# Neighbourhood attention in a two-layer encoder: both heads of a pair go through each query block together, and the keys wrap around

## The chip, the cores and the metric

The kernel runs on one core of one Trainium2 chip. The metric is the device time of one execution in microseconds (us). Three runs of the kernel before took 1664.18 to 1666.24 us, with a median of 1666.17 us. A profile of one execution goes with them, and its times are counted from the start of its span. Engines are named as in the profile: PE is TensorE's matrix multiplication and PEld its loading of weights (the stationary operand), DVE is VectorE, ACT ScalarE, POOL GpSimd, and SP the queue that issues most DMAs.

## The reference, cut to what matters

The model is an encoder of two layers over 512 tokens on a grid of 8 rows and 64 columns, with 1024 features in fp32. Layer 0 is neighbourhood attention and a dense SwiGLU, layer 1 latent attention (MLA) and a mixture of experts; each part is preceded by a modulated norm. The part at issue is the neighbourhood attention, with 16 heads of 64 features:

```python
q, k, v = split(h @ w_qkv); q = q * 64 ** -0.5
# every token sees 8 rows x 16 columns around its own, clamped at the border
s = q . k(window) + rpb[head, row offset, column offset]
p = softmax(s)            # over the 128 keys of the window
o = (p . v(window)) @ w_o
```

The modulation vectors of all parts come from `silu(c) @ w_ada + b_ada`, and a part of this product runs beside the attention.

## The kernel before, in words

Every fp32 matrix product with weights is made of three passes over a high and a low part of each operand ("hi" and "lo", lines 295 to 297, tiles `mm`, one accumulation of 24 matmuls of 512 columns for a projection). Weights arrive by DMA as `raw` tiles; ACT casts the high part (L195) and DVE subtracts for the low part (L198). DVE also sums the background product with `w_ada` (L225, `ada_acc`).

The tokens are ordered so that a window of 16 columns lies within 256 consecutive positions. So a query block of 128 positions needs 256 keys, and there are four query blocks (b = 0 to 3). The last block's keys wrap from position 511 to 0. Before the change a key tile `kT` has 640 columns, and POOL copies its first 128 columns behind the 512 (L749). Keys hold the high parts in partitions 0 to 63 and the low parts in 64 to 127. Queries `qH` hold the high part twice, the copy made by POOL (L741), and `qL` the low part over zeros, so two matmuls make a score.

Two heads form a pair, and there are eight pairs in four groups. The generator `attend(pair)` does, for head h and block b:

- PE: two matmuls of 256 columns into the score tile `s` (L682);
- DVE: adds bias and mask `mb` and takes the minimum along the row into `nm` (L685; scores carry a minus sign);
- ACT: exponential with the row sum `den` (L688); DVE: reciprocal (L689) and product (L690);
- PE: two transposes into `pt` (L693); ACT: a copy to `pT` (L695);
- PE: two matmuls `po` of a 128 x 64 block of V with `pT` (L697). Each stands in the trace as two records of 128 columns, so one head's block has four. Head 0 writes partitions 0 to 63 of `po`, head 1 partitions 64 to 127, so the two heads use different halves of PE's columns (form 128*64; all else in this stage has form 128*128).

All eight (head, block) steps of a pair come one after another in the code, head 0 first. POOL makes three `mb` tiles for each head (first, inner and last block, L674) from masks and the bias table `rb`, which SP loads (L628). Tiles live in pools with a fixed number of buffers: `s`, `pt`, `pT` and `mb` have two, `e`, `nm` and `den` three. The projections of the next group are issued between the pairs. Outside the start of this stage and the expert stage a scheduler sets the order of the instructions on each engine when the program is built: it sorts ready work by its own estimates, so attention steps and projection matmuls alternate on PE. On the chip each engine then works through its list in that order. After the last pair the output projection `na_o` (reading `oH` and `oL`) follows, then the dense SwiGLU. The latent attention of layer 1 has a product of the same form, `po` in L956, with 512 columns.

Of the kernel before, what the change touches and what calls it, by code (L numbers as in the profile page):

```python
# [13 lines left out]
OP = mybir.AluOpType  # L14
# [44 lines left out]
class Kernel:  # L59
# [20 lines left out]
    def add_slots(self, pool, n, big, raw_pool, n_raw):  # L80
        """slots besides the standing ones: for split weights n of pool and some of the big tiles, for loads n_raw and
        the halves of a big tile"""
        self.extra = pool
        self.slots = ["split"] * N_SPLIT + ["extra"] * n + ["big"] * big
        self.raw_slots = [raw_pool] * n_raw + [0, 1] + [self.rawp] * N_RAW
        self.turn_no, self.raw_no = N_FIRST - 1, -1
# [4 lines left out]
    # ---------------------------------------------------------------- weights  # L91
    def add_split(self, key, srcs, nk, cols, perm=None):
        """srcs: list of (dst column, DRAM AP [nk*128 rows, cols])."""
        self.jobs.append(("split", key, srcs, nk, cols, perm))
# [5 lines left out]
    def need(self, key, ahead=1):  # L100
        """Emit loads and splits up to `ahead` split jobs past `key`."""
# [25 lines left out]
    def preload(self, n, limit=None):  # L127
        """loads of the next n jobs"""
# [55 lines left out]
    def pieces(self, hi, lo, raw, early=0):  # L184
        """high and low parts, 1024 columns at a time; early: all high parts first, with a pause after them"""
# [25 lines left out]
    # -------------------------------------------------------------------- ada  # L211
# [20 lines left out]
    def ada_finish(self, acc, layer, which, m0, n):  # L232
        """sums over the partitions of acc [128, n * 128] -> columns m0 .. m0 + n of one modulation vector"""
# [16 lines left out]
    def emit_ada_cols(self, layer, which, b, raw=None):  # L250
        """256 columns of one modulation vector at a time"""
# [29 lines left out]
    # -------------------------------------------------------------- utilities  # L281
    def proj(self, hi, lo, m, act_hi, act_lo, nk, cols=P, tok=ALL):
        """psum[cols features, tokens] = W^T act, three exact passes."""
# [24 lines left out]
    def rstd_steps(self, accs, tok=ALL, eng=None):  # L308
        """pairs of [128, tokens], n -> self.rstd: PSUM [128, tokens] of each, 1/sqrt(sum over the partitions / n + eps)
        on every partition; pauses where TensorE would wait"""  # L310
# [42 lines left out]
    def norm_steps(self, xT, layer, which, hi, lo, tok):  # L353
        """hi + lo = modulated norm of the finished x"""
# [23 lines left out]
    def finish(self, xT, key, act_hi, act_lo, nk, layer, which, norm, ahead=None):  # L378
        """x += g * W^T act. The last outputs come in two halves of the tokens: the norm of one half runs under the
        products of the other."""  # L380
# [33 lines left out]
    # ------------------------------------------------------------------ setup  # L414
# [20 lines left out]
    def plan(self):  # L435
        """The order in which weights stream through the core."""
# [53 lines left out]
    def split_swapped(self, hi, lo, src):  # L490
        """last axis: exchange the members of each pair"""
# [29 lines left out]
    # ------------------------------------------------ neighbourhood attention  # L521
    def na_phase(self):
        nc, tc, d = self.nc, self.tc, self.d
        with ExitStack() as es:
# [15 lines left out]
            def gate():  # L540
                """sums for half the modulation of 256 features; loads run a fixed number of jobs ahead"""
                self.emit()
                self.preload(N_LOADS, N_GATES)
# [15 lines left out]
            def weights():  # L559
                """high parts now, the rest later"""  # L560
# [50 lines left out]
            vp = pool("na_v", 3)  # L611
            w2 = pool("na_w2", 2)
# [48 lines left out]

            def attend(pair):
# [3 lines left out]
                po = ps_o.tile([P, S], F32, name="po")  # L666
                for h in range(2):
                    rb = RB[pair][:, h, 248:249]
                    MB = []
                    for v in range(3):  # L670
                        mb = w2.tile([P, 256], F32, name=f"mb{v}")
# [6 lines left out]
                    for b in range(4):  # L678
                        z = qz[pair % NQ][h]
                        s = ps_s.tile([P, 256], F32, name="s")  # L680
                        for i in range(2):
                            nc.tensor.matmul(s, z[i][:, b * P:(b + 1) * P], kT[h][:, b * P:b * P + 256], start=i == 0, stop=i == 1)  # L682
                        e = w3.tile([P, 256], F32, name="e")
                        nm = w3.tile([P, 1], F32, name="nm")
                        nc.vector.tensor_tensor_reduce(e, s, MB[0 if b == 0 else (2 if b == 3 else 1)],  # L685
                                                       op0=OP.add, op1=OP.min, scale=1.0, scalar=3e38, accum_out=nm)
                        den = w3.tile([P, 1], F32, name="den")
                        nc.scalar.activation(e, e, AF.Exp, bias=nm, scale=-1.0, accum_out=den)  # L688
                        nc.vector.reciprocal(den, den)  # L689
                        nc.vector.tensor_scalar_mul(e, e, den)  # L690
                        pt = ps_t.tile([P, 2, P], F32, name="pt")
                        for t in range(2):
                            nc.tensor.transpose(pt[:, t], e[:, t * P:(t + 1) * P], self.ident)  # L693
                        pT = w2.tile([P, 2, P], F32, name="pT")
                        nc.scalar.copy(pT, pt)  # L695
                        for t in range(2):
                            nc.tensor.matmul(po[h * 64:h * 64 + 64, b * P:(b + 1) * P],  # L697
                                             V[:, (b + t) % 4, h * 64:h * 64 + 64], pT[:, t],
                                             start=t == 0, stop=t == 1)
                        yield  # L700
# [31 lines left out]
    def na_query(self, ps, z):  # L732
        """scaled queries of two heads, 64 positions on: the high parts twice, the low parts over zeros"""
# [9 lines left out]
    def na_key(self, ps, kp):  # L743
        """keys of two heads, high parts over low parts"""
        nc = self.nc
        kT = [kp.tile([P, 640], F32R, name=f"kT{h}") for h in range(2)]
        for h, k in enumerate(kT):
            self.split_piece(k[0:64, 0:512], k[64:128, 0:512], ps[h * 64:h * 64 + 64])
            nc.gpsimd.tensor_copy(k[:, 512:640], k[:, 0:128].bitcast(F32))  # L749
# [7 lines left out]
    # ------------------------------------------------------------- dense ffn  # L757
# [58 lines left out]
    # ------------------------------------------------ latent attention  # L816
    def mla_phase(self, xT, hH, hL, norm):
        nc, tc, d = self.nc, self.tc, self.d
        scale = 96.0 ** -0.5
        with ExitStack() as es:  # L820
# [20 lines left out]
            def latent(psums, tok):  # L841
                """norms of the compressed queries and keys"""
# [123 lines left out]
    # ------------------------------------------------ mixture of experts  # L966
# [13 lines left out]
    def router(self, small, hp, ps_a, ps_b, ps_c, cst):  # L980
        """generators that make the choice of experts from the halves of hT"""
# [41 lines left out]
        def first_rows(onehot, idx0, cnt):  # L1023
            """counts, places of the tokens among their experts' rows, and the rows of the first expert's first block"""
# [20 lines left out]
        def rest(R, C, T, idx0, ps_y):  # L1045
            """the rows of the first expert's second block, weights, every expert's rows, and the rows that each token
            reads back"""
# [72 lines left out]
    def moe_phase(self, xT, oH, oL):  # L1120
        nc, tc, d = self.nc, self.tc, self.d
        with ExitStack() as es:
# [84 lines left out]
            def part(x, ks, b, z, n=P):  # L1207
                """columns of block b: P high parts and P low parts, of few rows FEW and FEW"""
# [61 lines left out]
            def few_rows(ps, x, w, k0, k1, nk):  # L1270
                """high and low parts of at most FEW rows side by side: two passes, the sums of the low parts in partitions FEW on"""
# [27 lines left out]
            def overflow():  # L1299
                """slots past the first CAP of every expert, added to x_tok"""  # L1300
# [71 lines left out]
            def second_block(n, many, few):  # L1372
                """one of two ways for the rows past the first P"""
# [23 lines left out]
            def emit_to(n):  # L1397
                """splits of the first n jobs"""
# [28 lines left out]
            def flush():  # L1427
                """what ScalarE and VectorE still owe the second block"""
# [292 lines left out]
```

## Time and profile before

| | |
|---|---|
| median of three runs | 1666.17 us |
| profiled execution, span | 1664.0 us |
| granted TensorE clock, mean | 0.989 of full speed |
| PE busy | 1591.8 us (96%) |
| DVE busy | 1110.5 us (67%) |
| ACT busy | 825.3 us (50%) |
| POOL busy | 311.5 us (19%) |
| attention of layer 0 in the span | first score 77.2 us, last `po` 262.8 us |

The span runs from the first to the last instruction of the program; the median of the runs is 2.2 us above it. Matmuls are pipelined: a matmul of 512 columns lasts 0.39 us in the records while the next one starts 0.23 us after it. So the cost of PE work is read from start to start, not from durations, and a PE shown as busy can still lose time between two starts.

### The profile page before, as it was taken

The numbers are of one execution on the slowest core, as the hardware profiler recorded it, in microseconds if no ns is written. First come the engines' busy times: TensorE is split into PE (matmuls) and PEld (weight loads), VectorE is DVE, ScalarE is ACT, GpSimd is POOL, SyncE is SP. The second block draws the span as 40 slices with busy tenths as digits, with TensorE's granted clock in tenths as the row PEclk, the third lists the DMA queues.
The fourth block names the chain that finished last, engine by engine and source line by source line (L and its number), as shares of the span: only waits on it lengthen the run. The fifth ranks groups of instructions, "written<-read, shape, count | busy, mean of one in ns | idle before, by whom it ended". The sixth has DMA issues, their size and how long they took to land. (4 is left out here: it accounts for less than half of the span.)

```text
span 1664.0 us, 23262 instructions
## 1 busy us (share of the span) xinstructions
PE 1591.8 (96%) x7909; PEld 1258.5 (76%) x7909; DVE 1110.5 (67%) x1720; ACT 825.3 (50%) x1416; POOL 311.5 (19%) x275
## 2 busy tenths in 40 slices
PE   6899999999999999989999989999999999999996
PEld 4777778988888888966568677778887777777885
DVE  5777855755554624788874768755546888887765
ACT  3455543522122123477673657545446767766442
POOL 0342210001000000012100353212112333333310
PEclk9999999999999999999999989999999999999998
DMA  9635431357655523312213399858558999997851
GB/s 354 195 114 173 161 127 52 130 199 247 224 176 178 177 72 112 102 59 69 67 35 107 140 346 355 271 189 271 169 183 297 333 354 355 339 371 264 261 190 52
DMA packets 241210, 327.39 MB, mean 197 GB/s; under 512 B 9586, under 2 KB 191570, under 8 KB 240404
## 3 DMA queue, kind: packets, MB, share of 16 engines
q1 hardware_dynamic: 231072, 296.19, 53.5%
q0 software_dynamic: 5232, 18.09, 3.1%
q10 hardware_dynamic: 4740, 11.02, 1.8%
q8 instruction: 89, 1.46, 0.4%
q14 instruction: 77, 0.63, 0.1%
HBM read 308.75 MB, written 16.52 MB: 195 GB/s over the span
## 5 line engine op out<-in xcount | busy, mean ns | idle before, releaser
L198 DVE TENSOR_TENSOR lo<-raw,hi 128x1024 fp32r<-128x1024 f32 (+1 forms) x284 | 375.2, 1350 | 96.5 <-ACT hi L195 88.1
L195 ACT CAST hi<-raw 128x1024 fp32r<-128x1024 f32 (+1 forms) x319 | 318.5, 1045 | 220.7 <-PE mm L296 142.0
L296 PE MATMUL mm<-hL,hi 128*128 128x512 f32 x480 | 192.6, 401 | 0.0
L295 PE MATMUL mm<-hH,hi 128*128 128x512 f32 x480 | 191.3, 398 | 0.1
L297 PE MATMUL mm<-hH,lo 128*128 128x512 f32 x480 | 190.5, 397 | 0.0
L1235 PE MATMUL gu<-hi,he 128*128 128x512 f32 x360 | 144.5, 401 | 9.9 <-ACT act L1245 4.3
L198 POOL TENSOR_TENSOR lo<-raw,hi 128x1024 fp32r<-128x1024 f32 x39 | 101.9, 2613 | 237.0 <-ACT hi L195 182.5
L1237 PE MATMUL gu<-hi,he 128*128 128x512 f32 x360 | 141.3, 392 | 0.0
L1236 PE MATMUL gu<-lo,he 128*128 128x512 f32 x360 | 140.8, 391 | 0.0
L225 DVE SCALAR_TENSOR_TENSOR ada_acc<-raw,c_act,ada_acc 128x1024 f32<-128x1024 f32 x70 | 91.5, 1307 | 27.2 <-DMA raw<-in_w_ada_dram 26.6
L295 PEld LDWEIGHTS mm<-hH,hi 128*128 128x128 f32 x480 | 91.0, 190 | 21.4 <-issue 0.9
L296 PEld LDWEIGHTS mm<-hL,hi 128*128 128x128 f32 x480 | 90.9, 189 | 19.9 <-issue 1.5
L297 PEld LDWEIGHTS mm<-hH,lo 128*128 128x128 f32 x480 | 90.8, 189 | 19.5 <-issue 0.9
L1235 PEld LDWEIGHTS gu<-hi,he 128*128 128x128 f32 x360 | 67.6, 188 | 30.9 <-issue 7.5
L1245 ACT ACTIVATE act<-gu 128x256 f32<-128x256 f32 x56 | 21.5, 384 | 139.5 <-PE gu L1237 139.5
L1235 PE MATMUL y<-hi,a 128*128 128x512 f32 (+1 forms) x200 | 77.4, 387 | 2.1 <-PEq L1374 1.7
L1237 PEld LDWEIGHTS gu<-hi,he 128*128 128x128 f32 x360 | 67.6, 188 | 15.6 <-DVE he L209 0.4
L326 POOL TENSOR_TENSOR rs<-rs 128x2 f32<-128x2 f32 (+1 forms) x8 | 2.7, 336 | 408.3 <-DVE rs L324 408.3
L198 DVE TENSOR_TENSOR lo<-raws,hi 128x1024 fp32r<-128x1024 f32 x50 | 68.7, 1407 | 13.7 <-ACT hi L195 11.5
L1236 PEld LDWEIGHTS gu<-lo,he 128*128 128x128 f32 x360 | 67.7, 188 | 13.3
L1237 PE MATMUL y<-hi,a 128*128 128x512 f32 (+1 forms) x200 | 75.4, 377 | 0.0
L1236 PE MATMUL y<-lo,a 128*128 128x512 f32 (+1 forms) x200 | 75.3, 376 | 0.0
(400 smaller groups left out, 3695.9 us busy)
## 6 DMA issues: line engine op xcount, KB each, us to landing
raw<-in_moe_w_gu_dram SPq DMA_DIRECT2D x176, 512.0 KB
raw<-in_w_ada_dram SPq DMA_DIRECT2D x48, 1024.0 KB
raw<-in_moe_w_down_dram SPq DMA_DIRECT2D x37, 1024.0 KB
raws<-in_moe_w_gu_dram SPq DMA_DIRECT2D x48, 512.0 KB
raw<-in_ffn_w_gu_dram SPq DMA_DIRECT2D x22, 1024.0 KB
raw<-in_na_w_qkv_dram SPq DMA_DIRECT2D x12, 1024.0 KB
raws<-in_moe_w_down_dram SPq DMA_DIRECT2D x11, 1024.0 KB
raw<-in_ffn_w_down_dram SPq DMA_DIRECT2D x8, 1024.0 KB
```

The costliest lines, as they stand in the source:

```text
L195: nc.scalar.copy(hi[:, c], raw[:, c])
L198: eng.tensor_tensor(lo[:, c], raw[:, c], hi[:, c].bitcast(F32), op=OP.subtract)
L225: nc.vector.scalar_tensor_tensor(acc, raw[:, i], c, acc, op0=OP.mult, op1=OP.add)
L295: nc.tensor.matmul(ps, ah, bh, start=first, stop=False)
L296: nc.tensor.matmul(ps, ah, bl, start=False, stop=False)
L297: nc.tensor.matmul(ps, al, bh, start=False, stop=last)
L326: g.tensor_tensor(w, y, y, op=OP.mult)
L1235: nc.tensor.matmul(ps, xh, wh, start=first, stop=False)
L1236: nc.tensor.matmul(ps, xh, wl, start=False, stop=False)
L1237: nc.tensor.matmul(ps, xl, wh, start=False, stop=last)
L1245: nc.scalar.activation(a, ps[:, 0:256], AF.Silu)
```

## The change

`attend` now loops over the four blocks, and within a block over the two heads. The tiles of both heads lie side by side: `s`, `e` and `pt` are twice as wide, `nm` and `den` have two columns. One reciprocal (L698) and one copy to `pT` (L706) serve both heads; the other operations remain one for each head. In the product with V the order is now first half of the keys for head 0, for head 1, then second half for head 0, for head 1 (L709). All six `mb` tiles of a pair (L682) are made ahead of its blocks, and each has one buffer where there were two for three names. `e` has two double buffers. Keys have 512 columns; the last block reads columns 384 to 511 and then 0 to 127 through an access pattern (`keys`), and POOL's copies of 128 columns are gone. Docstrings and comment lines are blanked in the whole file, so that lines after 611 have other numbers.

```diff
+            w1 = pool("na_w1", 1)
             w2 = pool("na_w2", 2)
...
+            def keys(k, b):
+
+                if b < 3:
+                    return k[:, b * P:b * P + 256]
+                k = k[:, 3 * P:4 * P]
+                return bass.AP(tensor=k.tensor, offset=k.offset, ap=[list(k.ap[0]), [-3 * P, 2], [1, P]])
...
-                        mb = w2.tile([P, 256], F32, name=f"mb{v}")
+                        mb = w1.tile([P, 256], F32, name=f"mb{v}{h}")
...
-                    for b in range(4):
+                for b in range(4):
+                    s = ps_s.tile([P, 2, 256], F32, name="s")
+                    e = w2.tile([P, 2, 256], F32, name="e")
+                    nm, den = (w3.tile([P, 2], F32, name=n) for n in ("nm", "den"))
+                    for h in range(2):
                         z = qz[pair % NQ][h]
-                        s = ps_s.tile([P, 256], F32, name="s")
                         for i in range(2):
-                            nc.tensor.matmul(s, z[i][:, b * P:(b + 1) * P], kT[h][:, b * P:b * P + 256], start=i == 0, stop=i == 1)
...
+                            nc.tensor.matmul(s[:, h], z[i][:, b * P:(b + 1) * P], keys(kT[h], b), start=i == 0, stop=i == 1)
+                    for h in range(2):
+                        nc.vector.tensor_tensor_reduce(e[:, h], s[:, h], MB[3 * h + (0 if b == 0 else (2 if b == 3 else 1))],
+                                                       op0=OP.add, op1=OP.min, scale=1.0, scalar=3e38, accum_out=nm[:, h:h + 1])
+                        nc.scalar.activation(e[:, h], e[:, h], AF.Exp, bias=nm[:, h:h + 1], scale=-1.0, accum_out=den[:, h:h + 1])
+                    nc.vector.reciprocal(den, den)
+                    for h in range(2):
+                        nc.vector.tensor_scalar_mul(e[:, h], e[:, h], den[:, h:h + 1])
+                    pt = ps_t.tile([P, 2, 2, P], F32, name="pt")
+                    for h in range(2):
                         for t in range(2):
-                            nc.tensor.transpose(pt[:, t], e[:, t * P:(t + 1) * P], self.ident)
-                        pT = w2.tile([P, 2, P], F32, name="pT")
-                        nc.scalar.copy(pT, pt)
-                        for t in range(2):
+                            nc.tensor.transpose(pt[:, h, t], e[:, h, t * P:(t + 1) * P], self.ident)
+                    pT = w2.tile([P, 2, 2, P], F32, name="pT")
+                    nc.scalar.copy(pT, pt)
+                    for t in range(2):
+                        for h in range(2):
                             nc.tensor.matmul(po[h * 64:h * 64 + 64, b * P:(b + 1) * P],
-                                             V[:, (b + t) % 4, h * 64:h * 64 + 64], pT[:, t],
+                                             V[:, (b + t) % 4, h * 64:h * 64 + 64], pT[:, h, t],
                                              start=t == 0, stop=t == 1)
...
-        kT = [kp.tile([P, 640], F32R, name=f"kT{h}") for h in range(2)]
+        kT = [kp.tile([P, S], F32R, name=f"kT{h}") for h in range(2)]
         for h, k in enumerate(kT):
-            self.split_piece(k[0:64, 0:512], k[64:128, 0:512], ps[h * 64:h * 64 + 64])
-            nc.gpsimd.tensor_copy(k[:, 512:640], k[:, 0:128].bitcast(F32))
+            self.split_piece(k[0:64], k[64:128], ps[h * 64:h * 64 + 64])
```

PE's list before, in the second pair of the second group (the numbers behind names tell tiles apart; `x2` is two instructions; `po` reads one head's `pT` at a time):

```order
L297 MATMUL mm_1563<-hH_102,lo_1126 128x512
L697 MATMUL po_1410<-pT_1430,V_1197 64x128 x2
L697 MATMUL po_1410<-pT_1447,V_1197 64x128 x2
L693 MATMUL pt_1461<-ident_123,e_1454 128x128 x2
L682 MATMUL s_1508<-kT1_1096,qH11_100 128x256
L682 MATMUL s_1508<-kT1_1096,qL11_101 128x256
L682 MATMUL s_1525<-kT1_1096,qH11_100 128x256
L682 MATMUL s_1525<-kT1_1096,qL11_101 128x256
L697 MATMUL po_1410<-pT_1464,V_1197 64x128 x2
L693 MATMUL pt_1478<-ident_123,e_1471 128x128 x2
```

PE's list after the change, in the first pair of the first group:

```order
L709 MATMUL po_626<-pT_685,V_585 64x128 x4
L297 MATMUL mm_921<-hH_102,lo_548 128x512
L295 MATMUL mm_921<-hH_102,hi_547 128x512
L704 MATMUL pt_706<-ident_123,e_692 128x128 x4
L296 MATMUL mm_921<-hL_103,hi_547 128x512
L693 MATMUL s_839<-kT0_493,qH10_98 128x256
L693 MATMUL s_839<-kT0_493,qL10_99 128x256
L693 MATMUL s_839<-kT1_494,qH11_100 128x256
L693 MATMUL s_839<-kT1_494,qL11_101 128x256
L297 MATMUL mm_921<-hH_102,lo_548 128x512
L295 MATMUL mm_921<-hH_102,hi_547 128x512
L709 MATMUL po_626<-pT_711,V_585 64x128 x4
```

Scores of two heads, four transposes, and four `po` instructions now come as one piece each; 32 `po` pieces of four instructions stand where 64 pieces of two stood. Three matmuls of projections stand between the transposes into `pt_706` and the `po` that reads `pT_711`.

DVE's list before, at the border of two pairs in the second group (each head's block has its own reciprocal `den`):

```order
L685 ISA e_1437,nm_1438<-s_1434,mb1_1413 128x256
L685 ISA nm_1438 128x1
L689 RECIPROCAL den_1423<-den_1423 128x1
L685 ISA e_1454,nm_1455<-s_1451,mb1_1413 128x256
L685 ISA nm_1455 128x1
L740 SCALAR_TENSOR_TENSOR qL00_95<-mm_1370,qH00_94 64x64
L690 TENSOR_SCALAR e_1420<-e_1420,den_1423 128x256
L689 RECIPROCAL den_1440<-den_1440 128x1
L690 TENSOR_SCALAR e_1437<-e_1437,den_1440 128x256
```

DVE's list after the change, at the same border:

```order
L695 ISA e_1323,nm_1324<-s_1322,mb01_1316 128x256
L695 ISA nm_1324 128x1
L209 TENSOR_TENSOR oL_532<-po_1135,oH_506 128x448
L752 SCALAR_TENSOR_TENSOR qL00_95<-mm_1269,qH00_94 64x64
L698 RECIPROCAL den_1325<-den_1325 128x2
L695 ISA e_1349,nm_1350<-s_1348,mb10_1312 128x256
L695 ISA nm_1350 128x1
L209 TENSOR_TENSOR oL_532<-po_1135,oH_506 128x64
L752 SCALAR_TENSOR_TENSOR qL01_97<-mm_1269,qH01_96 64x448
L700 TENSOR_SCALAR e_1323<-e_1323,den_1325 128x256 x2
```

The reciprocal now stands behind the row minima of both heads and waits for both exponentials; the two products of a block follow each other.

## Rows read from the trace of the kernel before

**Rows 1.** The page: busy us (share of the span) and instructions of each engine.
```profile
PE 1591.8 (96%) x7909; PEld 1258.5 (76%) x7909; DVE 1110.5 (67%) x1720; ACT 825.3 (50%) x1416; POOL 311.5 (19%) x275
```
**Rows 2.** Windows, four attention stretches: length, busy PE PEld DVE ACT POOL, clock, DMA.
```profile
85.00:110.00 25.00, 24.94 (x151) 17.90 (x149) 18.58 (x64) 16.71 (x51) 14.09 (x15) 1.00 0.46 147
129.00:157.50 28.50, 28.10 (x166) 20.47 (x165) 22.61 (x61) 15.93 (x48) 7.76 (x11) 1.00 0.56 180
183.00:212.20 29.20, 28.80 (x170) 20.95 (x170) 22.96 (x62) 16.15 (x49) 7.74 (x11) 1.00 0.53 171
238.00:263.50 25.50, 25.50 (x153) 18.49 (x151) 14.62 (x57) 14.52 (x45) 2.94 (x4) 1.00 0.36 124
```
**Rows 3.** Waits of PE from 77 to 268 us: total, times, longest.
```profile
PE pt L693 <- DVE e L690: 0.6, 2, 0.3
```
**Rows 4.** Timeline of PE from 92 us: start, length, instruction, count.
```profile
92.04 0.39 PE L295 MATMUL mm<-hH,hi 128*128 128x512 f32 x1
92.26 0.39 PE L296 MATMUL mm<-hL,hi 128*128 128x512 f32 x1
92.58 0.65 PE L697 MATMUL po<-pT,V 128*64 128x128 f32 x4
93.16 0.39 PE L682 MATMUL s<-kT,qH 128*128 128x256 f32 x1
93.39 0.28 PE L682 MATMUL s<-kT,qL 128*128 128x256 f32 x1
93.50 0.38 PE L693 MATMUL pt<-ident,e 128*128 128x128 f32 x2
```
**Rows 5.** Timeline of PE: first `po` piece of the stage with its successor, and the last.
```profile
84.67 1.09 PE L697 MATMUL po<-pT,V 128*64 128x128 f32 x8
85.68 0.44 PE L693 MATMUL pt<-ident,e 128*128 128x128 f32 x2
...
262.82 0.65 PE L697 MATMUL po<-pT,V 128*64 128x128 f32 x4
```
**Rows 6.** Timeline of PE in the latent attention: `po` pieces and their successors.
```profile
741.26 1.07 PE L956 MATMUL po<-pT,V 128*64 128x512 f32 x2
742.27 0.50 PE L295 MATMUL s<-ktH,queries 128*128 128x512 f32 x1
...
751.18 3.65 PE L956 MATMUL po<-pT,V 128*64 128x512 f32 x14
754.76 0.44 PE L949 MATMUL pt<-ident,e 128*128 128x128 f32 x2
```
**Rows 7.** Lines, 77:268 (the last row 725:890): busy us, mean ns, idle before.
```profile
L674 POOL TENSOR_TENSOR mb<-masks,rb 128x256 f32<-128x256 f32 x42 | 36.1, 864 | 66.4 <-DVE nm L685 58.3 <-DVE den L689 7.0 <-DVE qL L740 0.6
L688 ACT ACTIVATE e<-e,nm 128x256 f32<-128x256 f32 x64 | 32.5, 508 | 14.3 <-DVE nm L685 13.7
L690 DVE TENSOR_SCALAR e<-e,den 128x256 f32<-128x256 f32 x64 | 28.9, 456 | 0.7
L695 ACT COPY pT<-pt 128x256 f32<-128x256 f32 x64 | 23.3, 372 | 28.1 <-PE pt L693 25.9 <-PE po L697 1.6
L688 ACT ACTIVATION_READ_ACCUMULATOR e<-e,nm 128x1 f32 x64 | 12.1, 189 | 0.0
L689 DVE RECIPROCAL den<-den 128x1 f32<-128x1 f32 x64 | 9.6, 153 | 1.7 <-ACT e L688 1.6
L749 POOL CAST kT<-kT 128x128 fp32r<-128x128 f32 x12 | 3.5, 294 | 21.5 <-DVE kT L209 21.3
L950 ACT COPY pT<-pt 128x512 f32<-128x512 f32 x64 | 37.1, 588 | 21.7 <-PE pt L949 15.8 <-PE po L956 5.1
```
**Rows 8.** Timeline of ACT: the copy that follows the transposes at 93.50 us.
```profile
93.98 0.37 ACT L695 COPY pT<-pt 128x256 f32<-128x256 f32 x1 [0.84 <-PE pt L693]
```
**Rows 9.** Waits of SP's queue from 60 to 268 us: total, times, longest.
```profile
SPq L628 <- POOL mb L674: 24.5, 6, 11.7
```
**Rows 10.** Windows, the expert stage to the end of the span.
```profile
900.00:1664.00 764.00, 723.46 (x3398) 580.24 (x3396) 532.79 (x638) 432.35 (x623) 208.49 (x126) 0.98 0.77 259
```

More of the change, by code (lines that the diff above doesn't have):

```diff
@@ L666, in attend @@
                 po = ps_o.tile([P, S], F32, name="po")
+                MB = []
                 for h in range(2):
                     rb = RB[pair][:, h, 248:249]
-                    MB = []
                     for v in range(3):
-                        mb = w2.tile([P, 256], F32, name=f"mb{v}")
+                        mb = w1.tile([P, 256], F32, name=f"mb{v}{h}")
                         bias = bass.AP(tensor=rb.tensor, offset=rb.offset,
@@ L677, in attend @@
                         MB.append(mb)
-                    for b in range(4):
+                for b in range(4):
[3 more added lines that the diff above has]
+                    for h in range(2):
                         z = qz[pair % NQ][h]
-                        s = ps_s.tile([P, 256], F32, name="s")
                         for i in range(2):
-                            nc.tensor.matmul(s, z[i][:, b * P:(b + 1) * P], kT[h][:, b * P:b * P + 256], start=i == 0, stop=i == 1)
[L683 to L691, printed above, removed]
-                        for t in range(2):
-                            nc.tensor.transpose(pt[:, t], e[:, t * P:(t + 1) * P], self.ident)
-                        pT = w2.tile([P, 2, P], F32, name="pT")
-                        nc.scalar.copy(pT, pt)
-                        for t in range(2):
@@ L697, in attend @@
+                    for t in range(2):
+                        for h in range(2):
                             nc.tensor.matmul(po[h * 64:h * 64 + 64, b * P:(b + 1) * P],
-                                             V[:, (b + t) % 4, h * 64:h * 64 + 64], pT[:, t],
+                                             V[:, (b + t) % 4, h * 64:h * 64 + 64], pT[:, h, t],
                                              start=t == 0, stop=t == 1)
-                        yield
+                    yield
                 for dst, a, b in ((64, 0, 448), (0, 448, 512)):
@@ L743, in na_key @@
     def na_key(self, ps, kp):
-        nc = self.nc
-        kT = [kp.tile([P, 640], F32R, name=f"kT{h}") for h in range(2)]
+        kT = [kp.tile([P, S], F32R, name=f"kT{h}") for h in range(2)]
         for h, k in enumerate(kT):
-            self.split_piece(k[0:64, 0:512], k[64:128, 0:512], ps[h * 64:h * 64 + 64])
-            nc.gpsimd.tensor_copy(k[:, 512:640], k[:, 0:128].bitcast(F32))
+            self.split_piece(k[0:64], k[64:128], ps[h * 64:h * 64 + 64])
         return kT
```

## The prediction

> **What bounds the kernel now.** I read the page first: PE is busy for 96% of the span [rows 1]. Then the windows of the four attention stretches, where two pairs each go through PE between the projections: PE is full in all of them at a granted clock of 1.00, its upper level of 2.4 GHz. DVE follows with 18.6 of 25.0, 22.6 of 28.5, 23.0 of 29.2 and 14.6 of 25.5 us, ACT with 14.5 to 16.7 us, and the DMA engines are half idle [rows 2]. The view of waits agrees: from 77 to 268 us PE waited 0.6 us in all, for DVE's product [rows 3]. So this stage costs what PE's list costs, and the list has to be read from start to start in PE's timeline.
>
> There the `po` pieces stand out. Around the one at 92.58 us, matmul 92.26 to second score 93.39 is 1.13 us. Undisturbed, that matmul takes 0.22 (92.04 to 92.26) and the first score 0.11 (93.39 to 93.50). The piece therefore costs 0.80 us [rows 4], of which 0.58 lies between its start and the next start; the rest is a late start and a late successor. A piece of eight records, two blocks of one head, takes 1.01 from start to start [rows 5], so four more records cost 0.43, 0.11 each. Of the 0.80, then, 0.43 is work and 0.37 the price of going from form 128*128 to 128*64 and back.
>
> **The change part by part.**
>
> *Fewer pieces.* From 84.67 to 262.82 us PE's timeline holds 55 pieces, 46 of four records and 9 of eight [rows 5]. They cost 46 x 0.80 + 9 x 1.23 = 47.9 us. The new list has 32 pieces, each with the four instructions of both heads, eight records.
>
> *Two heads at once.* What a new piece costs depends on whether the two halves of PE's columns work side by side. The rows of this stage that I show have one head's records, one after the other. The latent attention has pieces in the new order, heads alternating [rows 6]. One instruction alone, two records, takes 1.01 us. With a fixed part of 0.58 - 4 x 0.11 = 0.15, a record of 512 columns costs 0.43. Fourteen records in turn would need 0.15 + 14 x 0.43 = 6.2 us; they took 3.58, which is 0.15 + 8 x 0.43. So fourteen records went in eight turns: six pairs and two singles. A new piece of eight records then goes in four turns and costs what one of four costs now, 0.80. This gives 32 x 0.80 = 25.6 us, and the saving is 47.9 - 25.6 = 22.3 us. The bounds are 0.80 and, for no overlap at all, 1.23 [rows 5], which leaves 47.9 - 39.4 = 8.5 us. I take 0.80, since the rows of L956 are the same operation on the same two halves.
>
> The Trainium skill has a rule against this: TensorE: Matmul & The Clock Gate, Part 3 (Packing small matmuls, the mechanism), says that loading weights overlaps with running matmuls only when the row group differs. Both heads use all 128 rows, so by that rule the pieces would cost 1.23 and the saving would be 8.5 us. The trace of the latent attention disagrees, with 3.58 us against 6.2.
>
> *Scores and transposes.* Their number and columns on PE do not change, and the wrap-around reads the same 128 columns elsewhere. I take zero; were the split read of the last block slower by as much as the longest against the undisturbed score start (0.23 against 0.11 in rows 4), 32 reads would cost 3.8 us; a gain has no source, since no column is saved.
>
> *Wider copy.* ACT's copies fall from 64 x 0.372 to 32 x 0.588 us [rows 7], 5.0 us of ACT that PE does not see. But PE's `po` waits for a copy that is 0.22 us longer. From the second transpose (93.50 + 0.11) to the copy are 0.37 us [rows 4, 8]; with 0.59 and a release it makes 1.0 us that PE has to fill. In the piece shown in the list the fill is enough (three matmuls and four scores, 1.1 us). Counting the new list with these starts, 14 of the 32 pieces have about 0.93 us of fill, so 14 x 0.07 = 1.0 us is lost. Without any such fill it would be 32 x 0.22 = 7.0 us.
>
> *DVE.* 32 of 64 reciprocals of 0.153 us go [rows 7], 1.2 us in each stretch. The shared reciprocal adds a wait for both exponentials; behind it in DVE's order stand the next block's minima, the `oL` and `qL` parts, for which scores, transposes and the next projections wait. By the pieces (13, then 14 in each stretch) the first stretch would lose 5.3 and the others 5.7 us, so they would last 19.7, 22.8, 23.5 and 19.8 us, with DVE needing 17.4, 21.4, 21.8 and 13.4: 88, 94, 93 and 68%. With DVE's idle time shrinking freely nothing is lost. If it stays as it is (5.9 and 6.2 us in the second and third stretch), they last 27.3 and 28.0 and lose 4.5 us each. I take a third, 1.5 us each for these two and 0.5 each for the others, 4.0 in all, since PE has hardly waited for DVE so far [rows 3].
>
> *POOL and SP.* POOL loses the 12 copies of 0.294 us in this window and four ahead of it [rows 7]; PE does not wait for POOL [rows 3]. The single `mb` buffers let a pair's bias tile be made only when the pair before has used the same one; six tiles of 0.86 us, 5.2 us, fit into half a stretch of two pairs, and the queries' copies queued behind them belong to a pair later [rows 7]. I take zero, and if each of eight pairs waited for one tile, 6.9 us; there is no gain in it for PE. On SP the loads of `rb` and of weights change places; SP waited 24.5 us for POOL before such a load [rows 9], yet the DMA share is 0.36 to 0.56 [rows 2] and PE waits for no transfer [rows 3]. I take zero, at most the 11.7 us of the longest such wait.
>
> *To the end.* Behind the stage the lists read the same. PE is busy for 723 of the last 764 us at a DMA share of 0.77 [rows 10], and loads are held by buffers that PE's progress frees, so the time won should move the whole rest.
>
> The sum is 22.3 - 1.0 - 4.0 = 17.3 us. The profiled span becomes 1664.0 - 17.3 = 1646.7; the median lies 2.2 us above it, 1648.9, say 1649.
>
> **The rivals.**
>
> *No overlap.* The heads alternate, but PE finishes one half's records before the other's. The like is seen where eight records of one head took 1.01 [rows 5]; against it speak the fourteen [rows 6]. The saving is 8.5, less 1.0 for the copy: 1666.2 - 7.5 = 1658.7. DVE then has room. The rule of the Trainium skill's page on TensorE, told above, would give this case.
>
> *DVE becomes the bound.* The trace shows it at 79% in the two middle stretches [rows 2], and its in-order waits stay. For it speaks that its list is fixed beforehand; against it, that four head-scores can now be in flight where two could. The loss of 9.0 in the middle, 2.0 in the others and 1.0 for the copy leaves 10.3: 1655.9.
>
> *Slower: the second head's leg in every block.* `po` of head 0 now waits for head 1's exponential (0.51 + 0.19), its product (0.46) and the wider copy (0.22), 1.38 us later [rows 7]. At PE's transposes L704, 32 times, this costs 44 us if nothing fills it: 1666.2 - 22.3 + 44 = 1688. It decides from 22.3 / 32 = 0.70 us of wait in each block. For it speaks that PE's order is fixed; against it, that projection matmuls stand between and PE waited 0.6 us in the whole stage.
>
> **How the numbers follow.** Forecast 0.75, DVE 0.13, no overlap 0.07, slower 0.05. What a measurement of this kernel tells from no change is about 0.2%, 3.3 us; all cases but the last lie beyond it on the fast side, apart from a share of 0.03 of the DVE and the no-overlap case with further waits. So faster 0.92, same 0.03, slower 0.05. The range begins where nothing is lost, 1666.2 - 22.3 = 1643.9, and reaches past the DVE case to 1658, which leaves out most of the last two rivals.
>
> **What would show it.** PE's timeline after: 32 pieces of eight records, about 0.6 us from start to the next start, with records of the two heads starting together. At 1.0 us the overlap is missing. The windows show the stage some 17 us shorter and DVE at about 90% in the middle stretches; the waits of PE show the product (L700) and the copy (L706) with a few us. I am wrong if PE's waits in the stage exceed about 10 us, or if the rest of the span gives the time back.

## The result, and the profile after

The changed kernel takes 1646.37 us (median of four runs, 1644.11 to 1649.19), the kernel before beside it on the same chip 1665.18 us (1663.99 to 1666.24). The ratio is 0.9884 with a 95% interval of 0.9872 to 0.9895: 18.8 us sooner by the medians. Timed once more on another chip (E9 below) it took 1645.38 us against 1663.99, a ratio of 0.9883 (0.9867 to 0.9900). The profiled executions differ by 16.7 us in their spans (1664.0 and 1647.3); that of the change is the longest of its four runs.

The page after, in the form of [rows 1]:

```profile
PE 1572.5 (95%) x7909; PEld 1245.2 (76%) x7909; DVE 1107.1 (67%) x1688; ACT 819.9 (50%) x1384; POOL 310.9 (19%) x259
```

PE's busy time fell by 19.3 us with the same 7909 instructions: more of them overlap. DVE and ACT lost 32 instructions each and 3.4 and 5.4 us, POOL 16 and 0.6. PE's timeline shows where, at a place like that of [rows 4]:

```profile
92.06 0.39 PE L295 MATMUL mm<-hH,hi 128*128 128x512 f32 x1
92.38 0.66 PE L709 MATMUL po<-pT,V 128*64 128x128 f32 x8
92.97 0.39 PE L693 MATMUL s<-kT,qH 128*128 128x256 f32 x1
93.19 0.38 PE L704 MATMUL pt<-ident,e 128*128 128x128 f32 x2
```

Eight records now go from 92.38 to 92.97, 0.59 us, as long as four did (92.58 to 93.16 in [rows 4]); eight of one head took 1.01 [rows 5]. There are 30 such pieces, of 0.587 to 0.589 us each, and one in which two blocks meet. In the single records the two heads start 6 to 7 ns apart, and each such pair 0.11 to 0.16 us after the pair before.

The windows of the four attention stretches, in the columns of [rows 2]:

```profile
87.00:108.00 21.00, 20.76 (x149) 14.51 (x148) 19.39 (x57) 16.18 (x46) 12.12 (x14) 1.00 0.40 123
128.00:154.00 26.00, 25.38 (x171) 18.81 (x168) 21.64 (x58) 17.01 (x44) 10.25 (x12) 1.00 0.56 182
178.00:204.00 26.00, 25.35 (x171) 18.81 (x168) 21.77 (x58) 16.99 (x44) 10.23 (x12) 1.00 0.55 172
227.00:249.00 22.00, 21.79 (x160) 16.44 (x157) 14.31 (x54) 14.02 (x41) 3.75 (x4) 1.00 0.42 145
```

They are 13 us shorter in all, PE is busy for 98 to 99% of each, and DVE is at 83% in the two middle ones, 92% in the first. What PE waited for from 70 to 260 us (total, times, longest), to set beside [rows 3]:

```profile
PE s L693 <- DVE kT L209: 4.7, 1, 4.7
PE pt L704 <- DVE e L700: 1.1, 3, 0.5
PE po L709 <- ACT pT L706: 0.5, 1, 0.5
```

The last two lines look as if almost nothing were lost. The timeline of PE at one of these waits says otherwise:

```profile
184.08 0.39 PE L297 MATMUL mm<-hH,lo 128*128 128x512 f32 x1
184.30 0.39 PE L295 MATMUL mm<-hH,hi 128*128 128x512 f32 x1
185.21 0.63 PE L704 MATMUL pt<-ident,e 128*128 128x128 f32 x4 [0.52 <-DVE e L700]
```

Between the starts at 184.30 and 185.21 lie 0.91 us where 0.23 is usual: 0.68 us are lost, and the view counts 0.52, from the modelled end of the matmul. So I counted PE from start to start over equal work: from the first score to the last matmul that reads `oH`, 224.62 us before and 208.79 after (206.85 in E9). Each interval outside the pieces is split into its undisturbed length (the 20th percentile for the same neighbours in the list, over seven of the profiles) and the excess over it, which is put down to the matmul that starts late:

| us | before | after | E9 (the same kernel) |
|---|---|---|---|
| `po` pieces, start to next start | 36.36 | 18.71 | 18.72 |
| all other intervals, undisturbed | 184.63 | 180.00 | 180.00 |
| excess ahead of transposes (DVE's product) | 0.3 | 3.3 | 3.3 |
| excess ahead of `po` (the copy) | 0.7 | 1.6 | 1.4 |
| excess up to 84 us (first blocks) | 0.3 | 2.0 | 0.5 |
| other excess | 2.4 | 3.2 | 3.0 |

The first two rows give 17.65 + 4.63 = 22.3 us; 0.7 to 0.9 come back at `po` and 3.0 at the transposes. The lengths of the stage and of the pieces are plain differences of starts; the other rows hang on the choice of profiles and neighbours. Counted over other sets, the 4.63 came out between 3.6 and 4.6 and the 3.0 between 2.3 and 3.0. Three lines of 70 to 250 us go with it, as in [rows 7]: half as many copies and reciprocals, the copy as long as foreseen.

```profile
L700 DVE TENSOR_SCALAR e<-e,den 128x256 f32<-128x256 f32 x64 | 24.5, 423 | 0.5
L706 ACT COPY pT<-pt 128x512 f32<-128x512 f32 x32 | 18.6, 584 | 23.0 <-PE pt L704 22.5
L698 DVE RECIPROCAL den<-den 128x2 f32<-128x2 f32 x32 | 5.1, 158 | 5.5 <-ACT e L697 5.3
```

The first score starts at 77.23 us before and 77.32 after; the last `oH` matmul comes 15.74 us sooner, the last dense matmul and the last score of the latent attention 15.6 each, the last matmul of the experts' `gu` 15.80 and the end 16.67. So the gain is made in this stage and carried to the end.

The view shows a wait of 4.7 us ahead of the first score that the view of before has not. DVE (start, length, instruction, idle before) shows its origin:

```profile
71.80 1.29 DVE L225 SCALAR_TENSOR_TENSOR ada_acc<-raw,c_act,ada_acc 128x1024 f32<-128x1024 f32 x1 [4.78 <-DMA raw<-in_w_ada_dram]
73.12 1.41 DVE L209 TENSOR_TENSOR kT<-first,kT 64x512 fp32r<-64x512 f32 x2
76.48 0.69 DVE L209 TENSOR_TENSOR kT<-first,kT 64x512 fp32r<-64x512 f32 x1
```

The stage begins with four key tiles, two heads of two pairs. Three of their low parts (L209) stand behind a background sum whose load came late. The last of them ends at 77.17 us, and the first score starts 0.15 us later. The new order is not the reason: in ten of the thirteen profiles the first score starts 0.14 to 0.15 us after the last key tile, E2 with the old order among them. In the profiled execution before, the keys were ready at 75.45 us, and PE itself came later. PE's timeline shows a second price:

```profile
77.32 0.55 PE L693 MATMUL s<-kT,qH 128*128 128x256 f32 x1 [4.68 <-DVE kT L209]
77.67 0.41 PE L693 MATMUL s<-kT,qL 128*128 128x256 f32 x1
77.88 0.41 PE L693 MATMUL s<-kT,qH 128*128 128x256 f32 x1
```

The scores go at 0.21 us from start to start instead of 0.12. After the wait the granted clock is 0.50 in the windows from 77 to 81 us, the lower of its two levels (1.2 instead of 2.4 GHz), and 1.00 from 82 us on; this is the 2.0 in the table's fifth row. Before, PE lost as much at nearly the same place: 3.5 us ahead of a transpose of V at 70.7 us, and some twelve matmuls behind it at a granted clock of 0.50.

### The profile page after: what moved, and what is told of

Same layout as the page of the kernel before. It is cut to its first block, busy times and chain, and to the rows that moved or that the text cites. A ratio compares the mean times of both kernels' runs of the same rounds, so it can differ in the third digit from the quotient of the medians.

```text
span 1647.3 us, 23092 instructions
## 1 busy us (share of the span) xinstructions
PE 1572.5 (95%) x7909; PEld 1245.2 (76%) x7909; DVE 1107.1 (67%) x1688; ACT 819.9 (50%) x1384; POOL 310.9 (19%) x259
## 5 line engine op out<-in xcount | busy, mean ns | idle before, releaser
L198 DVE TENSOR_TENSOR lo<-raws,hi 128x1024 fp32r<-128x1024 f32 x50 | 73.4, 1501 | 14.6 <-ACT hi L195 12.9
```

What stands on the lines that cost most here:

```text
L198: eng.tensor_tensor(lo[:, c], raw[:, c], hi[:, c].bitcast(F32), op=OP.subtract)
```

## The experiments

E1 to E4 ran on one chip (before 1666.05 us, 15 runs), E5 to E8 on another (1665.31, 9 runs), E9 to E11 on a third (1663.99, 7 runs). Times are medians of four runs, of eleven in E2 and five in E7; ratios are to the kernel before on the same chip.

### E1: the heads in turn

```diff
-                    for t in range(2):
-                        for h in range(2):
+                    for h in range(2):
+                        for t in range(2):
                             nc.tensor.matmul(po[h * 64:h * 64 + 64, b * P:(b + 1) * P],
```

> The changed kernel with the two loops around the po instructions exchanged: both instructions of one head, then both of the other, so 32 pieces of eight records as before the edit, but records of the two heads no longer alternate. Theory (the gain needs both: fewer pieces and two heads at once): a piece takes about 1.0 us from start to next start (0.9 if the last record of one head still runs beside the first of the other) instead of 0.59, so 32 x 0.3 to 0.42 = 10 to 13.5 us are lost: 1656 to 1660. Rival (the number of pieces alone made the gain): 0.59 a piece stays, 1646 to 1647.

Measured: 1645.69 us (1643.70 to 1647.86), ratio 0.9884 (0.9867 to 0.9900), as the change itself. My theory fell. PE's timeline:

```profile
94.81 0.66 PE L709 MATMUL po<-pT,V 128*64 128x128 f32 x8
95.40 0.33 PE L704 MATMUL pt<-ident,e 128*128 128x128 f32 x1
```

Still 0.59 us. In the single records a second one starts 13 ns after the first, and both series go on at 0.11 to 0.16 us. The records do not name the head, but on one half no two start less than 0.10 us apart (E5). So the second series is the second head, though all four of its records stand behind the first head's in the list: PE takes up instructions for the other half of its columns while the first half is at work. Alternating the heads in the list is not needed, and it is too much to say of PE, as the description of the kernel does, that it works through its list in that order. The kernel before had shown the like at two of its nine pieces of eight records, those where head 0's last block meets head 1's first:

```profile
89.45 0.93 PE L697 MATMUL po<-pT,V 128*64 128x128 f32 x8
90.31 0.50 PE L297 MATMUL mm<-hH,lo 128*128 128x512 f32 x1
```

It takes 0.86 us (0.81 in the other, at 104.46 us) where eight of one head take 1.01, and the second head begins 0.27 us in. That left open whether the two halves matter at all (E5).

### E2: the keys with wrap-around, alone

```diff
-        kT = [kp.tile([P, 640], F32R, name=f"kT{h}") for h in range(2)]
+        kT = [kp.tile([P, S], F32R, name=f"kT{h}") for h in range(2)]
...
-            nc.gpsimd.tensor_copy(k[:, 512:640], k[:, 0:128].bitcast(F32))
```

The scores read `keys(kT[h], b)` as in the change; all else is the kernel before.

> The kernel before with the keys of 512 columns read with wrap-around and the copies of their first 128 columns on POOL gone, nothing else. Theory: PE's list is the same and it waits for POOL nowhere, the split read of the last block costs nothing: within 2 us of the kernel before, 1663 to 1667. Rival (the split read is slower, 0.06 us a score in 32 scores, or the queries' copies on POOL come earlier): 1 to 4 us up or down.

Measured: 1665.54 us (1663.41 to 1668.00), ratio 0.9999 (0.9990 to 1.0008). The split read and the copies on POOL cost nothing that these runs tell. In its profile the wait ahead of the first scores stands at the keys too, in a list whose PE order is that of the kernel before:

```profile
PE s L688 <- DVE kT L209: 3.1, 1, 3.1
```

### E3: rb of the third pair from POOL

```diff
-                        nc.sync.dma_start(rb[u * 64:u * 64 + 64, h], src)
+                        (nc.gpsimd if pair == 2 else nc.sync).dma_start(rb[u * 64:u * 64 + 64, h], src)
```

> The changed kernel with the four loads of rb of the third pair issued by POOL instead of SP, where they made the loads behind them wait until 64.7 us for bias tiles on POOL. Theory (the 4.7 us that PE waits ahead of its first score are the second head's keys, standing on DVE behind the sum ada_acc, which waits for its load): the load is issued about 57 us and lands by 66, DVE's wait of 4.8 us goes, the first score starts at about 73 at the full clock, and the end comes 4 to 7 us sooner: 1640 to 1643. Rival (the next load, of the weights of the next queries, is then what PE waits for, or the buffers hold the load up anyway): the wait moves to a projection and the time stays within 2 us of 1646.

Measured: 1645.15 us (1642.38 to 1647.40), ratio 0.9874 (0.9856 to 0.9893). The load did come earlier: DVE's sum is there without a wait,

```profile
68.05 1.28 DVE L225 SCALAR_TENSOR_TENSOR ada_acc<-raw,c_act,ada_acc 128x1024 f32<-128x1024 f32 x1
```

but PE then waits at the transposes of V, for a copy on ACT that stands behind the casts of the keys:

```profile
PE pv L657 <- ACT vt L654: 2.7, 1, 2.7
PE pt L704 <- DVE e L700: 2.1, 4, 0.6
```

The rival was right: the wait moved, as it had stood at the same transposes in the kernel before.

### E4 and E10: two blocks together

```diff
+                    last.append((b, pT))
+                    if b % 2:
+                        for c, w in last[::-1]:
...
```

What is left out are the four `po` instructions, now of block `c` and reading `w`.

> The changed kernel with the po instructions of two query blocks issued together (the later block first, so that the list keeps them in one piece): 16 pieces of 16 records instead of 32 of eight. Theory (0.37 us of each piece is the price of changing form and coming back, whatever its length): 16 x 0.37 = 5.9 us sooner, 1640 to 1642, a piece taking about 1.0 us from start to next start. Rival (the first block's weights wait for the second block's product, so pT and pt come free later and PE waits at transposes or copies): at least as much is lost as saved, 1645 to 1652, with waits of PE for DVE's product or ACT's copy of more than 5 us in the stage.

Measured: 1642.16 us (1641.30 to 1643.32), ratio 0.9860 (0.9844 to 0.9876). The second time, beside the changed kernel itself:

> The version with po of two blocks together, again beside the changed kernel. Theory (15 pieces fewer at 0.37 us, of which some 2 us come back as waits of transposes for DVE's product): 3 to 4.5 us faster than the changed kernel. Rival (the difference of the first comparison was chance between chips): within 1.5 us of it.

Measured: 1645.08 us (1643.79 to 1645.76), ratio 0.9884 (0.9867 to 0.9900). Of E4's profile, a piece of PE's timeline and PE's waits:

```profile
103.90 1.09 PE L712 MATMUL po<-pT,V 128*64 128x128 f32 x16
104.92 0.50 PE L296 MATMUL mm<-hL,hi 128*128 128x512 f32 x1
```
```profile
PE pt L704 <- DVE e L700: 3.4, 9, 0.9
PE pv L657 <- ACT vt L654: 2.7, 1, 2.7
PE s L693 <- DVE nm L695: 0.5, 1, 0.5
```

Sixteen records take 1.02 us, eight turns as worked out. The stage lasts 204.92 us (204.93 in E10) against 206.85 for the change in E9: pieces and their surroundings fall by 4.0 us (18.72 to 17.09 and 180.00 to 177.58), but 2.1 come back ahead of the transposes (3.3 to 5.4) and 1.4 at scores, with 1.1 saved ahead of `po`. So the price of a piece is there, though by this count it is 0.27 us for each of the 15 pieces fewer and not 0.37 (three of the 16 pieces end in a wait and last 1.26 us), and half of it goes into new waits. The net is 1.9 us in the stage. By the runs the difference was 4 us once (each beside the kernel before, on different chips) and 0.3 once; that this version is faster is likely, and not settled.

### E5: both heads on one half of the columns

```diff
+                nc.vector.memset(po[64:128], 0.0)
...
-                    for t in range(2):
-                        for h in range(2):
-                            nc.tensor.matmul(po[h * 64:h * 64 + 64, b * P:(b + 1) * P],
+                    for h in range(2):
+                        for t in range(2):
+                            nc.tensor.matmul(po[0:64, b * P:(b + 1) * P],
```

The loops stand in the order of E1. The second head's product overwrites the first's, so half of the attention output is left out, and DVE has eight fills of 0.49 us more.

> The changed kernel with the po instructions of both heads written to the first half of PE's columns, one head after the other; the second head's result overwrites the first's and the other half is set to zero, so the attention output is left out in part. Same number of pieces and records. Theory after the heads taken in turn made no difference (PE takes up instructions for the other column half ahead of the list's order, so the two halves run together whichever way they are listed): on one half nothing can run beside anything, a piece takes 1.0 us from start to next start instead of 0.59, and 32 x 0.42 = 13 us of the gain are gone: 1658 to 1661. Rival (records of a piece go fast for another reason, and the number of pieces alone makes the gain): 0.59 stays, 1645 to 1648.

Measured: 1658.68 us (1656.95 to 1659.61), ratio 0.9956 (0.9940 to 0.9971). PE's timeline:

```profile
89.51 1.09 PE L710 MATMUL po<-pT,V 128*64 128x128 f32 x8
90.53 0.44 PE L705 MATMUL pt<-ident,e 128*128 128x128 f32 x2
```

The piece takes 1.02 us, all pieces together 32.3 us instead of 18.7. That is 13.6 us more, and 12.3 to 13.3 us more in the time. Of the gain of 18.8, about two thirds come from the two halves at work together.

### E6: a copy for each head

```diff
-                    nc.scalar.copy(pT, pt)
+                    for h in range(2):
+                        nc.scalar.copy(pT[:, h], pt[:, h])
```

> The changed kernel with the copy of the transposed weights made once per head (64 copies of 256 columns) instead of once for both. Theory (the wider copy costs PE at most what the waits show, 0.5 us): no difference, 1644.5 to 1647, ACT 5 us busier. Rival by the prediction (14 of 32 pieces lack 0.07 us of fill for the wider copy): 1 us sooner, at the edge of what can be told; and if ACT had no room: 1 to 5 us later.

Measured: 1649.53 us (1649.49 to 1650.47), ratio 0.9903 (0.9888 to 0.9918): 3 to 4 us slower than the change. The rival's last branch held such a time, but for another reason, no room on ACT; ACT is busy for 17.46 of 26 us in the second of the four windows. PE's timeline and ACT's:

```profile
92.27 0.92 PE L710 MATMUL po<-pT,V 128*64 128x128 f32 x8
93.12 0.50 PE L297 MATMUL mm<-hH,lo 128*128 128x512 f32 x1
```
```profile
91.84 0.65 ACT L707 COPY pT<-pt 128x256 f32<-128x256 f32 x2 [0.61 <-PE pt L704]
```

This piece takes 0.85 us. In its records the first head begins at 92.27 and the second at 92.54, when its own copy is done, so they run side by side for only a part. Over the stage the pieces take 23.4 us, between the 18.7 of the change and the 32.3 of E5, while the transposes wait 0.9 less. The one wide copy, which I had put down as a cost, is what lets both heads start at once.

### E7: a reciprocal for each head

```diff
-                    nc.vector.reciprocal(den, den)
                     for h in range(2):
+                        nc.vector.reciprocal(den[:, h:h + 1], den[:, h:h + 1])
```

> The changed kernel with a reciprocal for each head, so that DVE does not wait for both exponentials before the first head's product. Theory (DVE has room, 83% in the middle stretches, and the shared reciprocal makes PE wait only about 1 us): within 1.5 us of the changed kernel, 1645 to 1648, for 32 reciprocals of 0.15 us more. Rival by the prediction (the shared wait costs 4 us): 2 to 4 us sooner, 1642 to 1644.

Measured: 1647.02 us (1644.78 to 1651.05), ratio 0.9891 (0.9877 to 0.9906). Two of PE's waits:

```profile
PE pt L704 <- DVE e L700: 1.4, 4, 0.6
PE pt L704 <- DVE den L699: 0.6, 2, 0.3
```

DVE's own waits ahead of the reciprocal from 78 to 250 us, of the change and of E7:

```profile
DVE den L698 <- ACT e L697: 5.3, 9, 1.3
DVE den L699 <- ACT e L697: 0.2, 1, 0.2
```

So the wait for both exponentials is there with one reciprocal (0.5 us in the kernel before) and all but gone with two. Yet counted from start to start the excess ahead of the transposes is 5.4 us, against 3.3 with one. That wait alone does not make the 3 us; E7 also lays 32 more reciprocals of 0.15 us on DVE, so what it would be without them is not shown.

### E8: more work for DVE

```diff
+                    nc.vector.tensor_scalar_mul(w1.tile([P, 256], F32, name="extra"), MB[1], 1.0)
```

> The changed kernel with one more product of 256 columns on DVE in each of the 32 blocks, of the bias tile into a tile that nothing reads, 0.42 us each, 13.5 us in all, 3.4 us in each of the four stretches. Theory (DVE is at 83% in the middle stretches of 26 us, so 4.4 us are free there): PE's waits for DVE rise by 1 to 4 us, 1647 to 1650. Rival (DVE is already the bound or its idle time cannot be used): all of it comes on top, 10 to 13.5 us: 1656 to 1660.

Measured: 1649.00 us (1646.37 to 1649.51), ratio 0.9894 (0.9879 to 0.9909). Two windows and PE's wait:

```profile
128.00:154.00 26.00, 25.20 (x171) 18.51 (x171) 23.82 (x64) 16.86 (x44) 9.24 (x12) 1.00 0.63 201
178.00:204.00 26.00, 25.17 (x168) 18.68 (x166) 23.78 (x65) 16.45 (x44) 9.23 (x12) 1.00 0.59 198
```
```profile
PE pt L705 <- DVE e L700: 4.2, 9, 1.6
```

The trace shows 0.49 us for each of the 32 products, 15.7 us of work on DVE, and they cost 2.6 to 3.6 us; the view's wait at the transposes is 4.2 us where the change has 1.1 and 1.3 (E9). DVE goes from 83 to 92% there, so its idle time can be used for the most part.

### E9: the changed kernel again

> The changed kernel itself, to stand beside the next two on one chip. All theories: 1645 to 1647. In its profile the wait at the first scores tells two readings apart: if the 4.7 us belong to the list they stand again; if the load's arrival in that one execution made them, the wait is some 2 to 3 us, at the scores or at the transposes of V, as in the run with the heads in turn, whose list is the same up to there.

Measured: 1645.38 us (1644.40 to 1645.93). PE's waits:

```profile
PE s L693 <- DVE kT L209: 3.2, 1, 3.2
PE pt L704 <- DVE e L700: 1.3, 4, 0.5
PE po L709 <- ACT pT L706: 0.3, 1, 0.3
```

The wait for the keys is 3.2 us, no score ran at the lower clock, and the first score starts at 75.82 us. In E1, whose list is the same up to there, it was 0.6 us at the keys and 2.1 at V. Its size belongs to the execution, by when the load lands; the first score started between 74.9 and 77.8 us in all profiles.

### E11: two blocks, the second head's product on ACT

```diff
-                        nc.vector.tensor_scalar_mul(e[:, h], e[:, h], den[:, h:h + 1])
+                        (nc.scalar.mul if h else nc.vector.tensor_scalar_mul)(e[:, h], e[:, h], den[:, h:h + 1])
```

> Two blocks together, and the second head's product with the reciprocal made by ACT instead of DVE (32 x 0.42 us off DVE, about 32 x 0.4 us onto ACT), so that the products of the two heads run side by side. Theory (what the two-block version still loses are transposes that wait for DVE's products): 1 to 3 us faster than two blocks alone, 1639 to 1641. Rival (ACT's list is as full, and the copy, the exponentials and the casts behind the product come later): the same or up to 4 us slower, with PE waiting for ACT's product or copy.

Measured: 1642.36 us (1639.68 to 1645.29), ratio 0.9868 (0.9849 to 0.9888). By the medians it is 3.0 us faster than the change and 2.7 than two blocks alone, but the intervals of the ratios overlap. The excess ahead of transposes stayed at 5.6 us, so it did not do what I made it for, although DVE, at 18.3 of 26 us in the middle windows, had half of the products less. Its stage (204.20 us) is 0.7 us shorter than in E10.

## Why the prediction was right, point by point

- **What bounds.** PE's list, read from start to start. Right: E2, E3 and E7 change other engines' work and leave the time within 2 us of what it was, and E8's 15.7 us on DVE cost 3.
- **Fewer pieces, two heads at once: 22.3 us.** Measured 22.3 (17.65 in the pieces, 4.63 around them), 0.59 us a piece. That it agrees to the tenth is luck, since the second part can be counted as 3.6 as well. E5 shows the part of the overlap (13.6 us in the pieces). The price of a change of form was put too high: 0.37 us in the forecast, 0.27 in E4. One condition was needless: that the heads alternate (E1). And two of the nine pieces of eight, taken at 1.23, held both heads already, so the 47.9 us is some 0.4 too much. By the rule of the Trainium skill that the prediction weighed (TensorE: Matmul & The Clock Gate, Part 3, loading overlaps only for other row groups) the pieces would have taken 1.01 us. The 0.59 in this trace speaks against it for halves of the columns, where all rows are shared. The Trainium skill's page TensorEngine Tiling (Array Packing), Key Properties, says that different tiles load weights and multiply in parallel. E1, where the list gave them one after the other, agrees (13 ns between the starts).
- **Wider copy: 1.0 us lost.** The excess ahead of `po` rose by 0.7 to 0.9, so the term has about its size. What I missed is the other side: two copies would cost 3 to 4 us (E6), since then the heads do not start together.
- **DVE: 4.0 us lost.** Measured 3.0 ahead of the transposes. The size was near, in part by luck: the third of the full loss that the forecast took had no row behind it. The reason is not settled. The wait that I named came (5.3 us on DVE), but without it the loss was 5.4 (E7). More load on DVE raises the waits (E8), and half of the products off DVE left the loss of two blocks as it was, 5.6 us after 5.4 (E11). Which instruction ahead of the transposes costs most was not tried. The shares of 88, 94, 93 and 68% in the stretches came out as 92, 83, 84 and 65%: I had let the stretches shrink by 22 us, and they shrank by 13, the rest of the gain lying between them.
- **Scores, POOL, SP: zero.** Right for scores and key copies (E2). The single `mb` buffers were not tried alone; the views of PE's waits show none for POOL.
- **Not foreseen.** The first `po` now needs the second head's product too. From the first score to the first `po` were 7.4 us before and are 8.4 in E1 and E9. In the profiled execution of the change it was 10.0, and the first `po` came 2.6 us later than before (84.67 to 87.30); 1.7 of it lie in the stage's first blocks at the lower clock. In E9 it came at 84.23, and the first blocks lost 0.2.
- **To the end.** 15.7 us at the end of the stage, 15.8 at the last `gu`, 16.7 at the end of the span: carried, as said. Where the last 0.9 come from was not looked into.

17.3 us were forecast; the stage gave 15.8 and 17.8 us in the two profiles of the change, the medians 18.8 and 18.6.

## What to carry to other kernels

Where two products use different halves of PE's columns, put them in the list as neighbours and make their inputs ready at one moment, with one copy for both: the order between them hardly matters, and inputs that came one after the other cost 4.7 of the 13.6 us that the overlap gives (E6). Count PE from start to next start over equal work before believing a list of waits: here the list showed 1.6 us at transposes and `po` where the count gave 4.9. Taking away a load's wait at the start of a stage may only uncover the next (E3).

## What had not been expected of the hardware

- PE runs ahead in its list across column halves: with two instructions, four records, of one half listed first, the other half's first record began 13 ns after theirs (E1), and 6 to 7 ns after when they alternate.
- The halves advance apart: when the second half's input came 0.27 us late, the first went on meanwhile, and the piece took 0.85 us, between 0.59 and 1.02 (E6, E5).
- After a transpose in a group, the next product starts 28 ns later where other transposes start 109 ns apart; the product itself then takes 0.31 us to the next start instead of 0.23. So nothing is won, but either interval alone misleads (both kernels).
